# Softmax attention: the filler of the first head pair queued from step 0 over 22 steps, in place of from step 4 over 18

## The chip, the cores and the metric

The kernel runs on one core of one Trainium2 chip. The metric is the device time of one execution in microseconds (us). The engines are PE (TensorE, matrix products; PEld is its weight load), DVE (VectorE), ACT (ScalarE), POOL (GpSimd) and SP (SyncE, which here only issues DMAs).

## The reference

Two layers of a sequence model with 1024 channels and 16 + 1024 = 1040 positions, all in float32. A layer has a gated linear attention (GLA, 4 heads), a softmax attention with a forget gate (FoX, 8 heads of 64), one output projection, and a gated feed-forward part with a short convolution. The change touches only the order of work in the softmax attention, which computes for each head

```python
c = jnp.cumsum(log_f, axis=1)                      # forget bias per position and head
logits = q @ k.T / sqrt(64) + c[q_pos] - c[k_pos]  # causal: -inf where k_pos > q_pos
o_fox = softmax(logits) @ v                        # then a norm per head
```

Its q, k and v are columns of one input projection, x_normed @ w_in. The GLA output is multiplied by a gate, silu(x_normed @ w_gr), from four further column tiles of the same projection.

## The kernel before

Activations lie transposed: channels on partitions, positions along the free axis. Each float32 product is three matmuls on values split into a high and a low part (`mm3`, lines 222 to 224). Most large tiles live in 33 fixed slots of 128 x 1040 floats, handed out from a first-in first-out free list (`Slots`); a new user of a slot waits until the old one has been read for the last time. Two more slots exist during softmax attention, "lent", and only the low parts of k (`kL`) take them.

The instructions are written in program order; the layer that builds the program then orders each engine's queue by priority and readiness, so an instruction of a later place in the program can run earlier than one ahead of it. Each engine works its finished queue in order.

Within a layer's attention the order of the program is: the GLA stage for two pairs of heads (`gla_steps`; the products of the first softmax pair run between its steps, and the weights of the second pair's q tile are loaded there: `coming`), then `fox`. `fox` (line 769) walks 72 steps: four head pairs p, and for each five groups of query tiles (7,8), (5,6), (3,4), (1,2), (0), two heads e, and the tiles of the group. So a pair has 18 steps; steps 0 to 17 are pair 0, steps 18 to 35 pair 1. Tiles 8 and 7 have the longest rows of scores, so the first steps of a pair are the heaviest.

One step n issues the scores of its query tile (`fox_scores`: products S at L658 and L659, the running minimum over S plus bias on DVE at L661, the exponential P on ACT at L673), the transposes of P two steps later (`fox_transposes`, L694, split again into high and low parts at L336 and L337), the product with v three steps later (`fox_av`, L720), and the fold and store four and six steps later. `cb` (line 807) holds the forget bias of the two heads of a pair over all positions on all partitions; it is loaded by SP at the first step of a pair (L809) and masked by POOL (L838).

Between these, `work.run` issues pieces of other products, the filler. `plan(p)` puts it into a queue: for p from 0 to 2 the q, k and v projections of pair p + 1 (`fox_products`) and gate p (`gr_products`), each a weight tile of 128 columns with 3 chunks of positions (344, 348, 348) and 24 matmuls a chunk; the results of the matmuls are in tiles named mm. For p = 3 it is the last gate, and for p = 4 the first part of the output projection. `fox_products` takes eight slots when it is called (qA, kA, kL and V, two each). From pair 1 on, a plan begins four steps into its pair, because the slots of the pair before come free only there. The steps at which plans begin are in the list `starts`; the filler of a plan is cut evenly over the steps to the next start:

```python
            if p_next < 5 and n == starts[p_next]:
                work.drain()
...
                work = plan(p_next)
                p_next += 1
            fill_us = work.left / max(starts[p_next] - n, 1)
```

Weights of a tile arrive in two halves of 4 x 128 columns: SP loads them (L180, tile raw), ACT makes the high part (L189), POOL or DVE the low part (L191). The buffers for high and low parts are three each, so the second half of the next tile waits for the first half of the current one to be used for the last time. The accumulators mm are two; the score accumulators S are three.

Of the kernel before, what the change touches and what calls it, by code (L numbers as in the profile page):

```python
# [131 lines left out]
def mm_us(n):  # L132
    return max(n / 2400.0, 0.107) + 0.0025


class Kern:
# [632 lines left out]
    def fox(self, lyr, ap, pp, qs, plan, mix3):  # L769

        nc = self.nc
        groups = ((7, 8), (5, 6), (3, 4), (1, 2), (0,))
        steps = [(p, g, e, ti) for p in range(4) for g in range(5) for e in range(2)
                 for ti in reversed(range(len(groups[g])))]
        first = [steps.index((p, 0, 0, 1)) for p in range(4)]
        starts = [f + 4 for f in first] + [first[3] + 8, len(steps) + 8]
        cbs, state, due = {}, {}, {}
        work, p_next = plan(-1), 0  # L780

        def at(slot, kind, f):
            due.setdefault((slot, kind), []).append(f)

        def run(slot, kind):
            for f in due.pop((slot, kind), ()):
                f()

        for n in range(len(steps) + 8):
            if p_next < 5 and n == starts[p_next]:  # L790
                work.drain()
                if 0 < p_next < 4:
                    self.fox_free(qs[p_next - 1])
# [3 lines that stand above are left out]
            for kind in ('av0', 'T0'):  # L797
                run(n, kind)
            if n < len(steps):
                p, g, e, ti = steps[n]  # L800
                tiles = groups[g]
                i = tiles[ti]
                rows = self.rows_of(i)
                if g == 0 and e == 0 and ti == 1:
                    if p:
                        self.slots.put(*cbs[p - 1])
                    cbs[p] = [self.slots.get(F32, "cb") for _ in range(2)]
                    for x in range(2):
                        nc.sync.dma_start(cbs[p][x][:, :T],  # L809
                                          self.cd[2 * p + x:2 * p + x + 1, :].to_broadcast([128, T]))  # L810
                        self.fox_mask(cbs[p][x], NT - 1)
                if e == 0 and ti == len(tiles) - 1:
                    state[p, g] = {"den": ap.tile([128, 2, 2], F32, tag="den", name="den", bufs=3)}
                st = state[p, g]
                if ti == len(tiles) - 1:
                    st[e] = {}
                with self.tc.high_priority(8):
                    Ps = self.fox_scores(e, i, qs[p], cbs[p][e], st["den"][:rows, ti, e:e + 1], ap, pp)
                if i:
                    self.fox_mask(cbs[p][e], i - 1)  # L820
                self.fox_schedule(lyr, at, n, p, e, ti, i, tiles, Ps, st, qs[p], ap, pp, mix3)
            parts = [c for c in "12" if (n, "av" + c) in due or (n, "T" + c) in due]
            work.run(fill_us / (1 + len(parts)))
            run(n, "store")
            run(n, "fold")
            for c in parts:
                run(n, "av" + c)
                run(n, "T" + c)
                work.run(fill_us / (1 + len(parts)))
        work.drain()  # L830
        self.slots.put(*cbs[3])
        self.fox_free(qs[3])
# [52 lines left out]
    def attention(self, lyr, nm, hsrc, chunks, feed):  # L885
        tc, nc, s = self.tc, self.nc, self.slots
        with tc.tile_pool(name=f"aps{lyr}", bufs=2, space=PSUM, reuse_waits="tile") as pp2, \
# [7 lines left out]
            with tc.tile_pool(name=f"gla{lyr}", bufs=1, reuse_waits="tile") as gp:  # L895
# [33 lines left out]
                work = Work()  # L929
# [21 lines left out]
            with tc.tile_pool(name=f"att{lyr}", bufs=2, reuse_waits="tile") as ap, \  # L951
                    tc.tile_pool(name=f"lent{lyr}", bufs=1, reuse_waits="tile") as lp:
                s.lent = s.add(lp, 2, f"a{lyr}_")
                box = {}
                KORD = (4, 5, 0, 1, 2, 3, 6)

                def plan(p):
                    w = Work()
                    if p < 0:
                        return w  # L960
                    if p < 3:
                        self.fox_products(lyr, p + 1, w, ap, pp, nm, qs[p + 1], None if p else coming["w"])
                        self.gr_products(lyr, p, w, ap, pp, nm)
                    elif p == 3:
                        self.mixing = True
                        land = box["land"] = [s.get(F32, f"h{k}") for k in range(KD - 1)]
                        for k in (4, 5, 0, 1, 2):
                            nc.gpsimd.dma_start(land[k][:, :T], self.mixd[k][:])
                        self.gr_products(lyr, 3, w, ap, pp, nm, land[3])

                        box["wo"] = {"src": self.wm[lyr, M_WO], "slots": None}
                        w.boxes.append(box["wo"])
                    elif p == 4:
                        land = box["land"]
                        for c0, n in reversed(CH):
                            nc.gpsimd.dma_start(land[6][:, c0:c0 + n], self.mixd[6][:, c0:c0 + n])
                        for x in nm["x"]:
                            s.put(*x)
                        s.put(nm["r"])
                        mix = box["mix"] = [(s.get(F32R, f"mh{k}"), s.get(F32R, f"ml{k}")) for k in range(KD)]  # L980
                        hT = box["hT"] = land

                        own = box["own"] = [s.get(F32R, "wl", (128, KD, 128)) for _ in range(2)]
                        boxes = [{"src": self.wm[lyr, M_WO + m], "work": w, "slots": own if m % 2 else None}
                                 for m in range(NSPLIT)]
                        boxes[0]["w"] = box["wo"]["w"]
                        w.boxes += boxes

                        def split(j):
                            c0, n = CH[j]  # L990
                            for k in KORD:
                                self.split(mix[k][0][:, c0:c0 + n], mix[k][1][:, c0:c0 + n], land[k][:, c0:c0 + n])
                            for m in range(NSPLIT):
                                nc.gpsimd.dma_start(hT[m][:, c0:c0 + n], hsrc[m][:, c0:c0 + n])
                        split(2)
                        boxes[1]["w"] = self.weights(boxes[1]["src"], own)

                        def ev(m):
                            def f(ps, c0, n):
                                h = hT[m][:, c0:c0 + n]  # L1000
                                nc.vector.tensor_tensor(out=h, in0=ps, in1=h, op=ALU.add)
                            return f

                        before = {(1, 2): lambda: split(1), (1, 1): lambda: split(0)}
                        for m, j in [(m, j) for j in (2, 1, 0) for m in (0, 1)] + [(m, j) for m in (2, 3) for j in (2, 1, 0)]:
                            c0, n = chunks[j]
                            w.add(self.unit(pp, boxes[m], boxes[m]["src"], KORD, mix, c0, n, ev(m), before.get((m, j))),
                                  len(KORD) * 3 * mm_us(n))
                    return w
                self.fox(lyr, ap, pp, qs, plan, lambda: box["mix"][KD - 1])  # L1010
                s.put(*box["own"])
                box["hT"].append(s.get(F32, "h7"))
# [752 lines left out]
```

## Time and profile before

| what | us |
|---|---|
| median of 3 runs | 2517.86 (2516.19 to 2520.93) |
| the profiled execution's own time | 2518.04 |
| its span, first to last instruction | 2516.3 |
| PE busy in the span | 2477.9 |
| DVE busy | 1767.2 |
| ACT busy | 1272.9 |
| POOL busy | 385.3 |

The profile gives busy time for each engine; instructions that only wait, branch or issue DMAs do not count. The ends of matmuls are modelled, so rows of PE overlap and the start of the next row tells more than the end of the last. Softmax attention runs from about 175 to 496 us in layer 0 and from about 1419 to 1740 us in layer 1.

### The profile page before, as it was taken

Reading aid. Unit: us, or ns where it says so; the run is one execution under the profiler, and the core shown is the slowest. Engines: PE = TensorE matmul, PEld = TensorE weight load, DVE = VectorE, ACT = ScalarE, POOL = GpSimd, SP = SyncE. Lnnn points to the kernel's source line nnn. Section 1 sums busy time; section 2 is a strip of 40 time slices with the busy share of each in tenths; the row PEclk is TensorE's granted clock in tenths of the full one; section 3 lists DMA queues with packets and bytes.
Section 4 is the critical chain, followed back from the end, with each engine's and each line's share of the span. In section 5 each row is a group of like instructions: output and inputs, shape, how many; then the busy total and the mean of one; then the engine's idle time right before and its main releaser. Section 6 shows DMA issues by size and latency. Waiting matters only on the chain.

```text
span 2516.3 us, 47049 instructions
## 1 busy us (share of the span) xinstructions
PE 2477.9 (98%) x18442; PEld 2383.8 (95%) x18442; DVE 1767.2 (70%) x3523; ACT 1272.9 (51%) x2733; POOL 385.3 (15%) x567
## 2 busy tenths in 40 slices
PE   9999999999999999999999999999999999999998
PEld 8999999999999999999999899999999999997786
DVE  8656777769877777853666666777798777787535
ACT  7346666636544445631443566665464444455312
POOL 2023433210000000100211234331100000001002
PEclk9999999999999999999999999999999999999999
DMA  3232134343322224763312222143433222258722
GB/s 133 67 88 74 44 92 133 118 130 97 119 81 81 77 77 146 193 170 106 107 57 69 74 80 78 58 153 109 142 105 101 76 79 78 80 166 186 194 56 74
DMA packets 118542, 260.94 MB, mean 104 GB/s; under 512 B 14880, under 2 KB 32544, under 8 KB 118320
## 3 DMA queue, kind: packets, MB, share of 16 engines
q1 hardware_dynamic: 93984, 182.79, 23.5%
q0 software_dynamic: 22464, 72.84, 10.4%
q8 instruction: 144, 2.36, 0.4%
q10 hardware_dynamic: 1872, 2.31, 0.3%
q14 instruction: 78, 0.64, 0.1%
HBM read 177.29 MB, written 67.81 MB: 97 GB/s over the span
## 4 chain that ended last, share of the span: by engine, by line
PE 81%; DVE 10%; ACT 4%; DMA 2%; issue 2%; SPq 0%; POOL 0%; DVEq 0%; ACTq 0%; POOLq 0%
PE up L222 11%; PE up L224 11%; PE up L223 11%; PE mm L222 7%; PE mm L224 7%; PE mm L223 7%; PE down L222 5%; PE down L223 5%; PE down L224 5%; PE av L720 3%; PE tr L694 2%; DVE S L661 1%; PE S L658 1%; ACT P L673 1%; PE S L659 1%
## 5 line engine op out<-in xcount | busy, mean ns | idle before, releaser
L222 PE MATMUL up<-x,hi 128*128 128x260 f32 (+1 forms) x2464 | 696.6, 283 | 0.0
L224 PE MATMUL up<-x,hi 128*128 128x260 f32 (+1 forms) x2464 | 695.9, 282 | 0.7 <-DVE x L1097 0.7
L223 PE MATMUL up<-x,lo 128*128 128x260 f32 (+1 forms) x2464 | 696.3, 283 | 0.0
L224 PEld LDWEIGHTS up<-x,hi 128*128 128x128 f32 x2464 | 465.3, 189 | 1.1 <-DVE x L1097 1.1
L222 PEld LDWEIGHTS up<-x,hi 128*128 128x128 f32 x2464 | 464.5, 189 | 0.4 <-DVE hu L1263 0.2
L223 PEld LDWEIGHTS up<-x,lo 128*128 128x128 f32 x2464 | 464.5, 189 | 0.1
L1073 DVE TENSOR_TENSOR lo<-raw,hi 128x512 fp32r<-128x512 f32 x364 | 247.7, 685 | 173.0 <-ACT hi L1072 172.7
L222 PE MATMUL mm<-xh,hi 128*128 128x348 f32 (+4 forms) x1056 | 362.7, 343 | 0.0
L224 PE MATMUL mm<-xl,hi 128*128 128x348 f32 (+4 forms) x1056 | 339.8, 322 | 0.0
L223 PE MATMUL mm<-xh,lo 128*128 128x348 f32 (+4 forms) x1056 | 339.4, 321 | 0.0
L1072 ACT CAST hi<-raw 128x512 fp32r<-128x512 f32 x364 | 223.6, 620 | 128.1 <-PE up L224 84.5
L222 PEld LDWEIGHTS mm<-xh,hi 128*128 128x128 f32 x1056 | 199.5, 189 | 5.2 <-issue 4.6
L223 PEld LDWEIGHTS mm<-xh,lo 128*128 128x128 f32 x1056 | 199.5, 189 | 0.7 <-issue 0.7
L224 PEld LDWEIGHTS mm<-xl,hi 128*128 128x128 f32 x1056 | 198.3, 188 | 0.4 <-issue 0.3
L189 ACT CAST hi<-raw 128x512 fp32r<-128x512 f32 (+2 forms) x168 | 97.4, 581 | 176.0 <-PE down L224 97.0
L223 PE MATMUL down<-ah,lo 128*128 128x260 f32 (+1 forms) x528 | 168.6, 319 | 0.4 <-DVE lo L191 0.3
L224 PE MATMUL down<-al,hi 128*128 128x260 f32 (+1 forms) x528 | 168.5, 319 | 0.0
L222 PE MATMUL down<-ah,hi 128*128 128x260 f32 (+1 forms) x528 | 168.2, 319 | 0.0
L673 ACT ACTIVATE P<-S,m 116x460 f32<-116x460 f32 (+2 forms) x224 | 124.8, 561 | 71.2 <-DVE m L661 67.6
L337 DVE TENSOR_TENSOR PT<-tr,PT 116x464 fp32r<-116x464 f32 (+3 forms) x240 | 122.8, 514 | 46.9 <-ACT PT L336 45.3
L1055 DVE TENSOR_TENSOR raw<-raw,raw 128x512 f32<-128x512 f32 x198 | 129.4, 684 | 17.2 <-DMA raw<-in_wd_dram 16.5
L1288 POOL DMA_DIRECT2D actd<-cv x44 | 23.6, 535 | 756.9 <-DVE cv L1287 735.9
(289 smaller groups left out, 5623.8 us busy)
## 6 DMA issues: line engine op xcount, KB each, us to landing
raw<-in_wm_dram SPq DMA_DIRECT2D x330, 256.0 KB, 2.7
raw<-in_wd_dram SPq DMA_DIRECT2D x64, 256.0 KB, 3.6
actd<-cv POOLq DMA_DIRECT2D x22, 520.0 KB, 3.0
actd<-cv POOLq DMA_DIRECT2D x22, 512.0 KB, 2.9
cb<-cd SPq DMA_DIRECT2D x16, 520.0 KB, 4.1
st<-actd SPq DMA_DIRECT2D x14, 520.0 KB, 4.9
st<-actd SPq DMA_DIRECT2D x14, 512.0 KB, 4.6
kA<-kA SPq DMA_DIRECT2D x24, 260.0 KB, 3.9
```

What stands on the lines that cost most here:

```text
L189: nc.scalar.copy(hi[:, :n, :], raw[:, :n, :])
L222: nc.tensor.matmul(ps, wh, xh[:, c0:c0 + n], start=first, stop=False, skip_group_check=more)
L223: nc.tensor.matmul(ps, wl, xh[:, c0:c0 + n], start=False, stop=False, skip_group_check=more)
L224: nc.tensor.matmul(ps, wh, xl[:, c0:c0 + n], start=False, stop=last, skip_group_check=more)
L337: nc.vector.tensor_tensor(out=lo, in0=src, in1=hi.bitcast(F32), op=ALU.subtract)
L658: nc.tensor.matmul(S[:rows, :n], q["qA"][e][:, qs], q["kA"][e][:, c0:k1], start=True, stop=False)
L673: nc.scalar.activation(P[:rows, :n], S[:rows, :n], AF.Exp, scale=-1.0, bias=m[:rows, nch - 1:nch], accum_out=(den if nch == 1 else d3[:row ...
L694: nc.tensor.transpose(tr[:w, 3 - j, :rows], P[:rows, o:o + w], id_)
L720: nc.tensor.matmul(av[:, a:b], w.rearrange("p a b -> p (a b)"), x, start=(t == ts[0] and part == 0 and i == 0), stop=(t == last and i == 1))
L1055: nc.vector.tensor_tensor(out=q[out][:, :nk, :], in0=q[a][:, :nk, :], in1=q[b][:, :nk, :], op=op)
L1072: nc.scalar.copy(hi[:, :nk, :], src[:, :nk, :])
L1073: nc.vector.tensor_tensor(out=lo[:, :nk, :], in0=src[:, :nk, :], in1=hi[:, :nk, :].bitcast(F32), op=ALU.subtract)
```

## The change

The list of starts begins with step 0 in place of 4, and the empty plan that filled the first four steps is gone. So the q, k and v projections of pair 1 and the first gate are queued from step 0 on and spread over 22 steps in place of 18. As `plan(0)` is called at the top of step 0, it takes its slots before `cb` of pair 0 does. Every later plan begins where it did.

```diff
         first = [steps.index((p, 0, 0, 1)) for p in range(4)]
-        starts = [f + 4 for f in first] + [first[3] + 8, len(steps) + 8]
+        starts = [0] + [f + 4 for f in first[1:]] + [first[3] + 8, len(steps) + 8]
         cbs, state, due = {}, {}, {}
-        work, p_next = plan(-1), 0
+        work, p_next = Work(), 0
...
                 def plan(p):
                     w = Work()
-                    if p < 0:
-                        return w
                     if p < 3:
```

## The prediction

> **What bounds the kernel now.** I read the page's busy line and its chain, then the stages of the first head pair, then the waits of the stage that stands out.
>
> ```profile
> PE 2477.9 (98%) x18442; PEld 2383.8 (95%) x18442; DVE 1767.2 (70%) x3523; ACT 1272.9 (51%) x2733; POOL 385.3 (15%) x567
> PE 81%; DVE 10%; ACT 4%; DMA 2%; issue 2%; SPq 0%; POOL 0%; DVEq 0%; ACTq 0%; POOLq 0%
> ```
>
> TensorE is the bound: 98% busy, 81% of the chain. A change that moves matmuls and removes none can gain only where TensorE waits. So the question is how much it waits in the 22 steps over which the filler is now spread ("filler": what `plan(0)` queues, 4 tiles x 3 chunks x 24 = 288 matmuls). A step begins with the first score matmul (L658) of a query tile. Steps 0, 4, 8, 18, 22 and 26 of layer 0 begin here:
>
> ```profile
> 175.54 0.45 PE L658 MATMUL S<-kA,qA 128*116 128x460 f32 x1
> 192.14 0.37 PE L658 MATMUL S<-kA,qA 128*116 128x460 f32 x1
> 207.33 0.37 PE L658 MATMUL S<-kA,qA 128*116 128x460 f32 x1
> 249.01 0.42 PE L658 MATMUL S<-kA,qA 128*116 128x460 f32 x1
> 268.10 0.37 PE L658 MATMUL S<-kA,qA 128*116 128x460 f32 x1
> 289.15 0.37 PE L658 MATMUL S<-kA,qA 128*116 128x460 f32 x1
> ```
>
> The stretches between them by windows (length, then busy time and count of PE, PEld, DVE, ACT, POOL, then clock, DMA share, GB/s); the second fence holds the filler alone (the tile mm):
>
> ```profile
> 175.50:192.10 16.60, 16.25 (x103) 14.13 (x102) 10.94 (x37) 10.95 (x33) 5.50 (x8) 1.00 0.24 70
> 192.10:207.30 15.20, 13.75 (x104) 12.72 (x103) 10.76 (x35) 10.80 (x33) 4.02 (x7) 1.00 0.01 2
> 207.30:249.00 41.70, 41.41 (x300) 40.81 (x299) 23.91 (x81) 24.64 (x74) 17.30 (x22) 1.00 0.34 95
> 268.10:289.10 21.00, 21.00 (x155) 20.68 (x154) 16.26 (x51) 14.58 (x42) 9.15 (x14) 1.00 0.22 69
> ```
> ```profile
> 175.50:192.10 16.60, 9.07 (x50) 7.84 (x50) 1.53 (x3) 0.00 (x0) 1.00 0.24 70
> 192.10:207.30 15.20, 3.37 (x16) 2.59 (x16) 0.00 (x0) 0.00 (x0) 1.00 0.01 2
> 207.30:249.00 41.70, 30.12 (x159) 25.11 (x159) 3.58 (x7) 0.00 (x0) 1.00 0.34 95
> 249.00:268.10 19.10, 11.93 (x63) 9.93 (x63) 1.02 (x2) 0.00 (x0) 1.00 0.16 55
> 268.10:289.10 21.00, 13.22 (x66) 10.37 (x66) 1.52 (x3) 0.00 (x0) 1.00 0.22 69
> ```
>
> Two things stand out. 50 of the 288 filler matmuls already run in steps 0 to 3, though the program queues none before step 4: the instructions are reordered ahead of their place when TensorE is free. And the hole is in steps 4 to 7: only 16 filler matmuls, TensorE idle 15.20 - 13.75 = 1.45 us, while the same four query tiles of the second pair (steps 22 to 25) carry 66 and show no idle time. Layer 1 has the same stage again, to 0.01 us of PE:
>
> ```profile
> 175.50:216.70 41.20, 39.10 (x270) 35.62 (x269) 27.70 (x92) 28.97 (x85) 14.82 (x21) 1.00 0.14 42
> 1419.30:1460.50 41.20, 39.11 (x271) 35.60 (x269) 27.73 (x92) 28.94 (x85) 14.84 (x21) 1.00 0.13 42
> ```
>
> In the hole the scores wait for the exponentials that free their banks, with nothing else ready (waits of steps 4 to 7, then the timeline):
>
> ```profile
> PEld S L658 <- ACT P L673: 1.5, 2, 0.9
> PE S L658 <- ACT P L673: 1.1, 2, 0.7
> ```
> ```profile
> 194.81 0.42 PE L658 MATMUL S<-kA,qA 128*116 128x348 f32 x1 [0.75 <-ACT P L673]
> 196.99 0.47 PE L658 MATMUL S<-kA,qA 128*116 128x460 f32 x1 [0.37 <-ACT P L673]
> ```
>
> **The change part by part, per layer.** *(a) The fill rate.* No instruction is added or removed; 288 matmuls are spread over 22 steps (13.1 a step) in place of 18 (16). Two of them back to back:
>
> ```profile
> 149.79 0.32 PE L223 MATMUL mm<-xh,lo 128*128 128x348 f32 x1
> 149.95 0.32 PE L224 MATMUL mm<-xl,hi 128*128 128x348 f32 x1
> ```
>
> They start 0.16 us apart. Without filler, steps 4 to 7 take 15.20 - 16 x 0.16 = 12.64 us; steps 22 to 25 take 21.00 - 66 x 0.16 = 10.44. The hole costs 2.2 us. After the change these steps get about 52 filler matmuls. By a straight line between the two stages (2.2 us over 66 - 16 = 50 matmuls, 0.044 us each) 36 more recover 1.6; if 13 a step already hide all, 2.2. I take 2.0, nearer the upper end, because the idle rows above are single waits under 0.8 us, which five matmuls cover. Steps 0 to 3 get 52 in place of 50: nothing.
>
> *(b) The thinner end.* Steps 8 to 21 had 159 + 63 = 222 and keep 14 x 13.1 = 183, so 39 fewer. The nearest rows with thin filler are in the fourth pair (steps 12 to 15 of it, all engines, then filler), and the heaviest steps of these are 20 and 21 (third fence):
>
> ```profile
> 474.90:488.90 14.00, 14.00 (x96) 13.77 (x96) 9.92 (x32) 6.94 (x22) 2.78 (x6) 1.00 0.33 115
> ```
> ```profile
> 474.90:488.90 14.00, 10.45 (x48) 8.21 (x48) 1.19 (x3) 0.00 (x0) 1.00 0.33 115
> ```
>
> ```profile
> 257.10:268.10 11.00, 10.88 (x74) 9.62 (x72) 10.68 (x33) 9.50 (x31) 3.31 (x6) 1.00 0.10 34
> ```
>
> In the fourth pair 48 matmuls in four steps keep TensorE busy throughout, so 12 a step is enough on light steps. In steps 20 and 21 the vector engine is busy 10.68 of 11.00. Steps 18 to 21 lose 11 matmuls (63 to 52): nothing if covered, 11 x 0.044 = 0.5 us by the line, up to 1.7 (39 x 0.044) if the line held for all 14 steps. I take 0.3.
>
> *(c) What the moved steps carry along.* Three more weight tiles on SP's queue and their casts (ACT) and remainders (POOL), the splits of q, k and v, six copies of k on SP, the gate's loads (SP) and stores (POOL). Two neighbouring rows of SP's queue, and the cast of the second half of the k tile's weights:
>
> ```profile
> 177.94 1.78 SPq L615 DMA_DIRECT2D gog<-ogd  x2
> 209.13 4.93 SPq L180 DMA_DIRECT2D raw<-in_wm_dram  x2
> ```
> ```profile
> 207.12 0.62 ACT L189 CAST hi<-raw 128x512 fp32r<-128x512 f32 x1
> ```
>
> SP issues nothing from 179.72 to 209.13, POOL is busy 4.02 of 15.20 us in steps 4 to 7, ACT 10.80: room is there. That weight half is cast at 207.12, once the q tile, still running in the hole, frees its buffer; with the q tile earlier, this comes earlier too. Cost taken: 0; without that room, at most the hole of (a) again, 2.2 us; a gain beyond (a) is excluded, since no work goes away.
>
> *(d) The buffers change hands.* The loads of the forget-bias tiles `cb`, the last matmuls that read the second GLA pair's values (L505), SP's next row, the first reduction that reads `cb`, the time that its loads take to land, and its mask on POOL:
>
> ```profile
> 116.36 0.33 SPq L809 DMA_DIRECT2D cb<-cd  x1
> 123.12 0.33 SPq L809 DMA_DIRECT2D cb<-cd  x1
> ```
> ```profile
> 167.73 0.67 PE L505 MATMUL u<-gv,kd 64*64 64x128 f32 x16
> ```
> ```profile
> 169.96 0.46 SPq L584 DMA_DIRECT2D kL<-kL  x1
> ```
> ```profile
> 180.83 0.64 DVE L661 CUSTOM_DVE_ANT_0 S<-S,cb 116x460 f32<-116x460 f32 x1
> ```
> ```profile
> DMA to landing us min/median/max: 3.7/4.1/5.5
> ```
> ```profile
> 120.67 0.43 POOL L838 TENSOR_TENSOR cb<-cb,mask 116x116 f32<-116x116 f32 x1 [4.33 <-DMA cb<-cd]
> ```
>
> `plan(0)` now takes its six slots before `cb` takes its two. The free list holds, oldest first, four slots of the first GLA pair and four of the second. So far `cb` got the two oldest and was loaded at 116 and 123 us; now it gets the last two, the second pair's values, free at 168.4. Issued behind the copy of 169.96, the load lands at 170.4 + 4.1 and is masked by 175.0; the first reduction that reads it runs at 180.83, which is 5.8 us of cover. Cost 0, upper end in the rivals. Behind a waiting `cb` load on SP stand weight loads for the filler, which the buffers hold back anyway.
>
> **Sum.** 2.0 - 0.3 = 1.7 us a layer, 3.4 for two layers. The profiled execution took 2518.04 (span 2516.3), 0.2 above the median 2517.86; so 2514.6 against its own time and 2514.5 at the median, 0.14% faster. About 0.2% (5 us) is what a measurement can tell from no change.
>
> The Trainium skill (Perfetto Trace Analysis, Identifying the Most-Contended Engine) says that busy time of matmuls is a bad measure of headroom and that weight-load busy time should be used. By matmuls the hole is 1.45 us, by weight loads 15.20 - 12.72 = 2.48; the sum (a) would be 2.9 us for two layers by the one and 5.0 by the other, and the difference from the second pair's steps lies between, nearer the page's measure.
>
> **The rivals.** *All is recovered.* Steps 4 to 7 give 2.2, and the other idle time in reach too: 16.60 - 16.25 = 0.35 in steps 0 to 3, 41.70 - 41.41 = 0.29 in steps 8 to 17; nothing is given back. 2.8 a layer, 2512.2. For it: the second pair runs with almost no idle. Against: it has 16 matmuls a step, not 13.
>
> *The reordering has done it already.* If waits follow the straight line, 1.6 recovered is given back as 1.7 later: 2518. For it: 50 matmuls sit in steps 0 to 3 unasked. Against: the thin steps of the fourth pair.
>
> *The bias comes late (slower).* If its load is placed behind the weight and gate loads on SP, that is after 177.94 + 1.78 = 179.72, it is ready at 184.3, 3.4 us after 180.83; with a landing of 5.5, 4.8. It decides from an issue later than 176.3 on. Every softmax of the layer starts that much later with no filler left for the delay, minus the 1.7 gained: 1.7 to 3.1 a layer, 2521.3 to 2524.1, middle 2522.7. For it: SP does wait in order, as the loads of 116 and 123 us did for their slots. Against: SP's last copy leaves at 169.96, just after the slots come free.
>
> **How the numbers follow.** Chances: forecast 0.37, all recovered 0.28, done already 0.14, late bias 0.21. The forecast's own bounds are 2513 to 2517. Faster by over 0.2% (below 2512.8): the second case and a little of the first, 0.30. Slower by over 0.2% (above 2522.9): half of the late bias, and waits of the kind of (c) and (d) where I took zero, 0.22. Within: 0.48. The range reaches into both outer cases: 2511.5 to 2522.7.
>
> **What would show it.** In the changed profile the score matmul of step 8 should lie 3.8 us later after the first score (36 x 0.16 - 2.0) and that of step 22 1.7 us earlier; steps 4 to 7 should carry about 52 filler matmuls and idle under 0.4 us; steps 26 on should last as before; `cb` should be issued near 170 us, and L661 begin within 1 us of 180.8. Wrong is the prediction if `cb` is issued after 176, if steps 18 to 21 idle by more than 1 us, or if the reordering changes another stage.

## The result and the profile after

The changed kernel takes 2521.28 us (median of 13 runs, 2518.74 to 2526.64) against 2517.09 us (13 runs) before: a ratio of 1.0018, with a 95% interval of 1.0011 to 1.0026. By the medians it is 4.2 us slower. The forecast was 2514.5, so its sign was wrong, though 2521.28 lies inside the stated range. The profiled execution took 2522.45 us, with a span of 2520.4; of before, 2518.04 and 2516.3.

The page of the changed kernel, busy line and chain by engine:

```profile
PE 2476.4 (98%) x18442; PEld 2381.5 (94%) x18442; DVE 1773.2 (70%) x3523; ACT 1272.9 (51%) x2733; POOL 386.6 (15%) x567
PE 48%; issue 30%; DVE 13%; ACT 4%; DMA 3%; POOL 1%; SPq 0%; DVEq 0%; POOLq 0%; ACTq 0%
```

TensorE does the same work in the same time; what grew is the time around it. (30% of the chain now goes by "issue", time in which the engine waited for nothing that the profile shows. It says nothing of the loss: it is 30% in e15 too, the fastest of the kernels below.)

The stages of layer 0 in the changed kernel: steps 0 to 3, 4 to 7, 8 to 17, 18 to 21, and step 22 (length, then busy time and count of PE, PEld, DVE, ACT, POOL, then clock, DMA share, GB/s); the second fence holds the filler alone in the second to fourth of these stages.

```profile
174.24:192.95 18.71, 16.73 (x107) 14.78 (x105) 11.18 (x37) 11.25 (x34) 6.92 (x11) 1.00 0.30 92
192.95:212.39 19.44, 18.85 (x140) 18.32 (x138) 13.04 (x38) 13.91 (x39) 8.65 (x12) 1.00 0.10 30
212.39:250.34 37.95, 37.55 (x274) 36.48 (x272) 23.84 (x76) 21.23 (x67) 12.14 (x18) 1.00 0.36 91
250.34:267.56 17.22, 17.01 (x114) 15.39 (x113) 15.36 (x52) 13.44 (x46) 4.86 (x8) 1.00 0.19 59
267.56:274.48 6.92, 5.76 (x43) 5.42 (x42) 6.92 (x21) 4.35 (x14) 3.20 (x5) 1.00 0.45 147
```
```profile
192.95:212.39 19.44, 11.18 (x51) 8.11 (x51) 1.02 (x2) 0.00 (x0) 1.00 0.10 30
212.39:250.34 37.95, 25.70 (x132) 20.76 (x132) 2.56 (x5) 0.00 (x0) 1.00 0.36 91
250.34:267.56 17.22, 10.21 (x51) 8.11 (x51) 1.02 (x2) 0.00 (x0) 1.00 0.19 59
```

The change does what it says: steps 4 to 7 carry 51 filler matmuls in place of 16, and their idle time falls from 1.45 to 19.44 - 18.85 = 0.59 us. But two idle times are new: 18.71 - 16.73 = 1.98 us in steps 0 to 3, where it was 0.35, and 6.92 - 5.76 = 1.16 us in step 22, where it was none. The waits of PE in the two places (for whom; us, times, longest) name two different causes:

```profile
PE S L659 <- DMA kL<-kL: 1.8, 1, 1.8
PE S L658 <- ACT P L673: 1.2, 1, 1.2
```

**The first wait: the low part of k comes late.** The queue of SP and the first scores in the changed kernel:

```profile
165.29 0.46 SPq L584 DMA_DIRECT2D kA<-kA  x1
167.15 0.87 SPq L809 DMA_DIRECT2D cb<-cd  x1
168.26 0.78 SPq L584 DMA_DIRECT2D kL<-kL  x1
169.14 0.54 SPq L809 DMA_DIRECT2D cb<-cd  x1
```
```profile
174.24 0.45 PE L658 MATMUL S<-kA,qA 128*116 128x460 f32 x1
176.43 0.44 PE L659 MATMUL S<-kL,qA 128*116 128x460 f32 x1 [1.75 <-DMA kL<-kL]
```

The two `cb` loads now stand on either side of the last copy of kL. The copy is issued no later than before (6.0 us ahead of the first score; before, 175.54 - 169.96 = 5.6), but it lands much later. The transfers that the profile lists for the window of 168 to 178 us, with KB each and median us from issue to landing, in the changed kernel, and then the same copy in the kernel before:

```profile
cb<-cd SPq DMA_DIRECT2D x2, 520.0 KB, 8.2
raw<-in_wm_dram SPq DMA_DIRECT2D x3, 256.0 KB, 4.9
kL<-kL SPq DMA_DIRECT2D x1, 260.0 KB, 8.0
```
```profile
kL<-kL SPq DMA_DIRECT2D x1, 260.0 KB, 4.4
```

Before, the copy landed at 169.96 + 4.4 = 174.4 us, about 1.2 us ahead of the first score's start. That cover is what the change used up. In layer 1 the changed kernel shows the same wait with 0.3 us: there the copy landed after 6.4 us, and after 3.4 in the kernel before.

**The second wait: VectorE is behind at step 22.** The first reduction of step 22 (L661, 460 columns, on VectorE) frees the way for the exponential P that PE waits for. The first row is from the kernel before, the second from the changed one:

```profile
271.18 0.63 DVE L661 CUSTOM_DVE_ANT_0 S<-S,cb 116x460 f32<-116x460 f32 x1
```
```profile
271.73 0.63 DVE L661 CUSTOM_DVE_ANT_0 S<-S,cb 116x460 f32<-116x460 f32 x1
```

From the first score it starts 271.18 - 175.54 = 95.6 us later before, and 271.73 - 174.24 - 1.75 = 95.7 after, without the kL wait: VectorE arrives at the same moment, whatever PE had saved by then. It is busy all 6.92 us of that step.

Over steps 0 to 23 the changed kernel needs 105.31 us in layer 0 and 103.79 in layer 1, where the kernel before needs 103.06 and 102.98. Steps 24 to 35 are the same to 0.05 us. That is 3.1 us of the 4.1 by which the two spans differ. The rest has no one place: from step 36 of layer 0 to the first score of layer 1 (the rest of the attention, the feed-forward part and the next layer's start) it takes 3.6 us more, the time up to the first score is 1.3 us shorter and the time behind step 36 of layer 1 also 1.3. In the repeat below neither of the first two shows.

### The profile page after: what moved, and what is told of

It is laid out like the page before. It is cut to its first block, busy times and chain, and to the rows that moved or that the text cites. A ratio compares the mean times of both kernels' runs of the same rounds, so it can differ in the third digit from the quotient of the medians.

```text
span 2520.4 us, 47039 instructions
## 1 busy us (share of the span) xinstructions
PE 2476.4 (98%) x18442; PEld 2381.5 (94%) x18442; DVE 1773.2 (70%) x3523; ACT 1272.9 (51%) x2733; POOL 386.6 (15%) x567
## 4 chain that ended last, share of the span: by engine, by line
PE 48%; issue 30%; DVE 13%; ACT 4%; DMA 3%; POOL 1%; SPq 0%; DVEq 0%; POOLq 0%; ACTq 0%
PE mm L222 7%; PE mm L223 7%; PE mm L224 7%; PE down L223 5%; PE down L222 5%; PE down L224 5%; PE av L720 3%; PE tr L694 2%; DVE S L661 1%; PE S L658 1%; DVE x L1095 1%; PE S L659 1%; DVE cv L1254 1%; DMA kL<-kL 1%; DVE lo L1071 1%
```

## The experiments

All ratios are to the kernel before, measured beside the run on the same chip, with 95% intervals. "Steps 0 to 23" is the time from the first score of step 0 to that of step 24.

| run | median, us | ratio to before | steps 0 to 23, layer 0 / 1, us | steps 24 to 35, us |
|---|---|---|---|---|
| kernel before | | | 103.06 / 102.98 | 52.06 / 52.02 |
| changed, first profile | 2521.28 | 1.0018 [1.0011, 1.0026] | 105.31 / 103.79 | 52.11 / 51.99 |
| e0, changed again | 2521.88 | 1.0016 [1.0007, 1.0025] | 104.73 / 104.84 | 52.10 / 51.99 |
| e1, bias slots first | 2517.13 | 0.9999 [0.9990, 1.0008] | 103.52 / 103.54 | 52.04 / 51.97 |
| e2, before with late bias | 2521.12 | 1.0014 [1.0004, 1.0023] | 104.12 / 104.92 | 52.11 / 51.95 |
| e3, start at third step | 2516.74 | 0.9999 [0.9990, 1.0008] | 102.76 / 102.98 | 52.10 / 52.11 |
| e4, before, lean gate | 2515.78 | 0.9994 [0.9985, 1.0003] | 103.09 / 102.88 | 52.05 / 51.96 |
| e5, e1 with lean gate | 2515.52 | 0.9993 [0.9984, 1.0002] | 101.97 / 101.92 | 52.06 / 51.96 |
| e7, bias from POOL's queue | 2528.77 | 1.0042 [1.0028, 1.0055] | 109.78 / 109.90 | 52.13 / 51.97 |
| e8, gate second, 19 steps | 2523.73 | 1.0022 [1.0014, 1.0031] | 111.56 / 108.73 | 48.55 / 48.61 |
| e10, last gate chunk later | 2516.73 | 1.0000 [0.9991, 1.0009] | 102.77 / 102.80 | 52.40 / 52.35 |
| e11, splits of steps 0 to 21 on VectorE | 2516.98 | 0.9999 [0.9990, 1.0008] | 103.55 / 103.63 | 52.03 / 51.99 |
| e12, one bias late | 2520.17 | 1.0011 [1.0002, 1.0020] | 103.66 / 103.32 | 52.09 / 52.04 |
| e14, e1 with the turn's splits on VectorE | 2513.51 | 0.9989 [0.9980, 0.9998] | 101.95 / 101.88 | 52.22 / 52.18 |
| e15, e14 and e10 together | 2512.31 | 0.9985 [0.9976, 0.9993] | 102.18 / 102.18 | 51.89 / 51.85 |
| e16, before with the turn's splits on VectorE | 2517.54 | 1.0003 [0.9994, 1.0011] | 103.30 / 103.03 | 51.88 / 51.83 |
| e14 again | 2515.16 | 0.9991 [0.9982, 1.0000] | 102.03 / 101.92 | 52.27 / 52.21 |

### Once more (e0)

The changed kernel without an edit.

> The changed kernel once more, for a second profile. Theory (contention and VectorE): the time lies 3 to 5 us above the kernel before; steps 0 to 23 of layer 0 are 1.5 to 2.5 us longer than before, those of layer 1 0.3 to 1.0 us, and the wait of the first kL product (L659) of layer 0 is there again, 1 to 2 us. Rival (chance of one profile): the kL wait of layer 0 is below 0.5 us in this profile, and the longer stretches of the feed-forward part lie elsewhere than in the first profile.

The loss is there again, 1.0016. The kL wait is 1.2 us in layer 0 and 1.3 in layer 1, the stall of step 22 is 1.18 us in both. The longer stretch between the two softmax attentions is not there again: the window of 1000 to 1200 us, first in the first profile of the changed kernel, then in this one.

```profile
1000.00:1200.00 200.00, 195.06 (x1611) 194.44 (x1611) 115.37 (x146) 78.52 (x118) 14.77 (x18) 0.99 0.59 153
```
```profile
1000.00:1200.00 200.00, 197.27 (x1643) 196.65 (x1642) 117.76 (x149) 79.89 (x119) 14.74 (x18) 1.00 0.60 155
```

So what happens in this part differs from run to run, and the loss of steps 0 to 23 stays (3.5 us here, 3.1 in the first profile). How it falls on the two layers varies: 1.7 and 1.9 us here, 2.3 and 0.8 there; for layer 1 at most 1.0 us had been expected.

### The two parts of the change apart (e1, e2)

e1 keeps the new start and gives `cb` its old slots back:

```diff
         cbs, state, due = {}, {}, {}
+        cbs[0] = [self.slots.get(F32, "cb") for _ in range(2)]
...
                     if p:
                         self.slots.put(*cbs[p - 1])
-                    cbs[p] = [self.slots.get(F32, "cb") for _ in range(2)]
+                        cbs[p] = [self.slots.get(F32, "cb") for _ in range(2)]
```

e2 keeps the old start and gives `cb` the late slots:

```diff
-                    cbs[p] = [self.slots.get(F32, "cb") for _ in range(2)]
+                    late = [i for i in self.slots.free if i not in self.slots.lent][-2:] if p == 0 else [None] * 2
+                    cbs[p] = [self.slots.get(F32, "cb", first=[x]) for x in late]
```

> The changed kernel, but pair 0's two bias tiles take their slots ahead of the work's allocations, as in the kernel before, so that only the fill rate differs from the kernel before. Theory (the late bias loads delay the kL copies, and the slots' order spreads further): most of the loss is gone; the kL wait is below 0.3 us in both layers, the time lies between 1.0 us below and 1.5 us above the kernel before, and steps 0 to 23 are within 0.6 us of before in each layer. Rival A (the moved start itself costs: gate and products in the early steps): as slow as the changed kernel, 3 to 5 us above before. Rival B (the prediction as it was: the fill rate is worth 1.7 us per layer once the bias is early): 2.5 to 4 us below before.

> The kernel before, with its start at the fifth step, but pair 0's bias tiles take the last two free slots, those that the second gated-linear pair gives back; nothing else changes. Theory: 1.0 to 3.5 us above before, with a kL wait in step 0 of 0.3 to 2 us per layer. Rival A (the moved start itself costs): within 0.5 us of before. Rival C (the slots' order, through the feed-forward part's buffers too, is the whole of it): 3.5 to 5 us above before, with longer stretches in the feed-forward part as in the changed kernel.

e1 is as fast as the kernel before, e2 as slow as the changed kernel. Steps 0 to 23 of layer 0 and of layer 1, first in e1, then in e2:

```profile
176.12:279.64 103.52, 100.81 (x703) 95.21 (x701) 74.34 (x234) 67.95 (x208) 35.75 (x52) 1.00 0.26 72
1420.90:1524.44 103.54, 100.83 (x703) 95.14 (x701) 74.37 (x234) 67.93 (x208) 35.77 (x52) 1.00 0.26 73
```
```profile
175.96:280.08 104.12, 101.03 (x703) 95.34 (x702) 72.00 (x234) 68.00 (x207) 36.46 (x53) 1.00 0.26 77
1423.43:1528.35 104.92, 100.83 (x704) 95.30 (x703) 71.72 (x234) 67.97 (x207) 36.54 (x53) 1.00 0.25 76
```

In e2 the two layers lose 1.06 + 1.94 = 3.0 us, nearly all of it in step 0 (PE idles 1.0 and 2.1 us there, 0.23 before), and the time says 1.0014. In e1 step 0 idles 0.24 us as before, and the kL copy lands after 4.4 us again. (In layer 1 of e2 the profile puts PE's wait of 1.9 us down to a split on POOL. The product that waits reads nothing of that split; it reads kL, whose copy was issued at 1417.58 us and landed 8.0 us later, at 1425.6, and the product started at 1425.74.) So the late bias is the loss, and rival A of these two runs (the moved start) falls. Rival C (the slots' order acting through the feed-forward part) needs a second look, for in e2's profile the stretch from step 36 of layer 0 to layer 1's first score is 2.5 us longer than before. But it is 3.7 us longer in e10 below, where the bias is early, and no longer at all in e0, where it is late. It does not go with the slots, so this rival falls too. And the fill rate alone, which the prediction had priced at a gain of 1.7 us a layer, costs 0.5 us a layer in the trace: rival B falls too.

### How the loads delay the copy (e7, e12)

e7 is the changed kernel with pair 0's bias loads on another queue; e12 is the kernel before with one late bias tile.

```diff
-                        nc.sync.dma_start(cbs[p][x][:, :T],
-                                          self.cd[2 * p + x:2 * p + x + 1, :].to_broadcast([128, T]))
+                        (nc.sync if p else nc.gpsimd).dma_start(
+                            cbs[p][x][:, :T], self.cd[2 * p + x:2 * p + x + 1, :].to_broadcast([128, T]))
```
```diff
-                    cbs[p] = [self.slots.get(F32, "cb") for _ in range(2)]
+                    last = [i for i in self.slots.free if i not in self.slots.lent][-1] if p == 0 else None
+                    cbs[p] = [self.slots.get(F32, "cb", first=[i]) for i in (None, last)]
```

> The changed kernel with pair 0's two bias loads issued from POOL's queue in place of SP's; they still take the last two slots and still start late. Theory (the loads share the DMA engines' time with the kL copies, whoever issues them): the wait of the first kL product stays, 0.5 to 2 us per layer, and the time stays 2.5 to 5 us above before. Rival (the order of issues on SP makes the kL copies late): the wait is gone and the time is within 1.5 us of before.

> The kernel before, with only one of pair 0's two bias tiles on a late slot; it is issued ahead of the last kL copy, the other one stays early. Theory (the late loads and the kL copy share the DMA engines' time, in proportion to the bytes under way): the kL wait of step 0 is 0 to 1.0 us per layer, less than with both late (0.8 and 1.9 us), and the time 0 to 2 us above before. Rival (any load issued between the kL copies costs the whole wait): 0.8 to 2 us per layer, as with both.

On another queue it gets worse, not better: 1.0042. PE's wait in layer 0 of e7 and its transfers issued from 168 to 178 us:

```profile
PE S L659 <- DMA kL<-kL: 4.0, 1, 4.0
```
```profile
cb<-cd POOLq DMA_DIRECT2D x2, 520.0 KB, 10.1
raw<-in_wm_dram SPq DMA_DIRECT2D x2, 256.0 KB, 8.5
kL<-kL SPq DMA_DIRECT2D x1, 260.0 KB, 10.3
```

The copy is issued at the same place on SP with no bias load around it, and yet takes 10.3 us. So the order of issues on SP isn't the cause. What fits is that the transfers share what moves them. The Trainium skill says so (DMA: Bandwidth & Descriptors, Issuing engines are not separate DMA queues): whoever issues a transfer, all run on the same 16 engines and interleave. The trace agrees, and shows more than that: with the loads on the other queue the copy takes 2.3 to 3.3 us more than the 7.0 to 8.0 that it takes with them on SP.

The time rose by more than the 2.5 to 5 us that had been expected, and the copy alone doesn't make it. Steps 0 to 3 of layer 0 in e1, then in e7:

```profile
176.12:193.06 16.94, 16.67 (x108) 14.71 (x105) 11.18 (x37) 11.23 (x34) 6.08 (x9) 1.00 0.20 68
```
```profile
175.89:199.11 23.22, 19.19 (x108) 17.23 (x106) 11.34 (x37) 11.26 (x34) 6.94 (x11) 0.85 0.27 78
```

The same 108 matmuls keep PE busy 2.5 us longer, because the clock granted to TensorE is lower: 0.50 from 180 to 186 us, right behind the wait of 4.0 us, and 1.00 again from 188 us on. Layer 1 shows it again, with a wait of 4.8 us and 1.7 us more busy time. After the waits of at most 2 us in the changed kernel, e0 and e2 the granted clock stays at 1.00. So e7's loss is part wait and part clock, and only the wait bears on the queues.

With one late load (e12) the wait of layer 0 is 0.5 us and the copy lands after 6.6 us:

```profile
kL<-kL SPq DMA_DIRECT2D x1, 260.0 KB, 6.6
```

That is between 4.4 with none and 7.0 to 8.0 with two. In layer 1 it lands after 4.7 us, and the idle time of step 0 is 0.3 us, against 0.25 before. The rival of e12 (any load between the copies costs the whole wait) falls. Its time, 1.0011 or some 3 us, is more than the 2 us expected at most and than the 0.9 us that steps 0 to 23 show; its interval reaches down to 1.0002, and the rest isn't explained.

### A start at the third step (e3)

```diff
-        starts = [0] + [f + 4 for f in first[1:]] + [first[3] + 8, len(steps) + 8]
+        starts = [2] + [f + 4 for f in first[1:]] + [first[3] + 8, len(steps) + 8]
```

> The changed kernel with the start at the third step in place of the first (20 steps in place of 22), so that the bias tiles take their slots first by themselves. Theory: like the run with the bias slots first, between 1.0 us below and 1.5 us above before, with some 56 filler products in steps 4 to 7 and a stall of about 1 us on P in step 22. Rival A: 1.5 to 3.5 us above before, between the two kernels. Rival B: 2.5 to 4 us below before.

Here `cb` takes its slots first by itself, and the time is that of the kernel before. Steps 4 to 7 get only 37 filler matmuls and still idle 1.54 us, as the plan queued in step 2 runs from step 5 on; step 22 idles 0.0 and 0.16 us, not about 1. So the expectation of the time held and that of its make-up did not: little is won early, and little lost at step 22.

### What eats the gain at step 22 (e4, e5)

Both leave three VectorE instructions out of the first gate; e4 is the kernel before with that, e5 is e1 with that. (The last lines only give the result its right sign again.)

```diff
-            nc.vector.tensor_scalar(out=e, in0=x, scalar1=-87.0, scalar2=None, op0=ALU.max)
-            nc.scalar.activation(e, e, AF.Exp, scale=-1.0)
+            if h:
+                nc.vector.tensor_scalar(out=e, in0=x, scalar1=-87.0, scalar2=None, op0=ALU.max)
+            nc.scalar.activation(e, e if h else x, AF.Exp, scale=-1.0)
...
-            nc.vector.scalar_tensor_tensor(out=e, in0=e, scalar=1.0, in1=y, op0=ALU.add, op1=ALU.mult)
-            nc.vector.scalar_tensor_tensor(out=y, in0=e, scalar=-2.0, in1=y, op0=ALU.add, op1=ALU.mult)
+            if h:
+                nc.vector.scalar_tensor_tensor(out=e, in0=e, scalar=1.0, in1=y, op0=ALU.add, op1=ALU.mult)
+                nc.vector.scalar_tensor_tensor(out=y, in0=e, scalar=-2.0, in1=y, op0=ALU.add, op1=ALU.mult)
...
-            nc.vector.scalar_tensor_tensor(out=to, in0=y, scalar=-1.0, in1=og, op0=ALU.mult, op1=ALU.mult)
+            nc.vector.scalar_tensor_tensor(out=to, in0=y, scalar=-1.0 if h else 1.0, in1=og, op0=ALU.mult, op1=ALU.mult)
```

> The kernel before, with three VectorE instructions left out of the first gate of each layer (the clamp L621 and the two that refine the sigmoid, L626 and L627), nine per layer; the gate's last digits are thereby not the reference's. It is the base for the next run. Theory (PE sets the pace of steps 18 to 23 in the kernel before): steps 0 to 23 within 0.3 us of the kernel before in each layer, step 22 without PE idle, the time 0 to 1 us below before. Rival (VectorE already sets that pace in the kernel before): steps 18 to 23 are 1 to 3 us shorter per layer.

> The changed kernel with the bias slots first and the same three VectorE instructions left out of the first gate. Theory (in the kernel with the bias slots first, what steps 0 to 21 win is lost in step 22, where VectorE is behind with the gate's chain and PE waits for P): the PE idle of step 22 falls from 1.18 us to below 0.3 us, steps 0 to 23 take 102.0 to 102.7 us per layer, and the time is 1.0 to 2.5 us below the lean kernel before. Rival (the stall of step 22 is the thinner filling itself, a score product that waits for a bank whoever drains it): step 22 still idles 0.8 us or more and steps 0 to 23 still take 103.3 us or more.

Step 22 in e1, and then in e5:

```profile
267.70:274.60 6.90, 5.72 (x44) 5.39 (x42) 6.90 (x21) 4.36 (x14) 3.18 (x5) 1.00 0.47 147
```
```profile
267.30:272.86 5.56, 5.56 (x43) 5.51 (x42) 5.32 (x18) 5.18 (x17) 3.62 (x6) 1.00 0.38 109
```

In the kernel before, less VectorE work changes nothing (103.09 and 102.88 us): there PE sets the pace. In e5 the stall is gone and steps 0 to 23 take 101.97 and 101.92 us, 1.0 to 1.1 below e4. So what steps 0 to 21 win is real, and VectorE takes it back at step 22. The 1.0 to 2.5 us that e5 was expected to gain on e4 do not show in the medians (2515.78 and 2515.52); this reading rests on the trace.

### Remedies for step 22 (e8, e10, e11)

e8 puts the gate's tile second among the four tiles and the work on 19 steps, and issues what was put off to a next tile at the change of plans (`flush`); e10 puts the rest of the gate's third chunk off to the next tile; e11 moves the weight splits (L191) issued in steps 0 to 21 from POOL to VectorE. All three have the bias slots first.

```diff
-        starts = [0] + [f + 4 for f in first[1:]] + [first[3] + 8, len(steps) + 8]
+        starts = [0, first[1] + 1] + [f + 4 for f in first[2:]] + [first[3] + 8, len(steps) + 8]
...
+                self.flush()
...
+                        if p == 0:
+                            w.q[3:] = w.q[-3:] + w.q[3:-3]
+                            w.boxes.insert(1, w.boxes.pop())
```
```diff
+            def rest():
...
+            if h == 0 and c0 + n == T:
+                self.later.append(rest)
+            else:
+                rest()
```
```diff
-            eng = nc.gpsimd if self.att and not self.mixing else nc.vector
+            eng = nc.gpsimd if self.att and not self.mixing and not self.early else nc.vector
...
+            self.early = n < starts[1]
```

> A candidate: bias slots first, start at the first step, the gate's tile moved from fourth to second place in the work of pair 0, and this work spread over 19 steps, so that the products of pair 1 are still in time and the gate's VectorE chain lies in steps 4 to 9, where VectorE is some 70% busy. Theory (the gate's chain in steps 18 to 22 ate the gain): step 22's PE idle is below 0.3 us, steps 0 to 23 take 101.6 to 102.6 us per layer, the time is 1 to 3 us below before. Rival (any spread gives back at the thinner or later end what it wins): steps 0 to 23 at 102.9 us or more and a time within 1 us of before; the idle has moved to another step.

> The changed kernel with the bias slots first, and of the first gate's third chunk everything behind its evacuation (L621 to L631) is put off to the next tile's first chunk; nothing is left out. Theory (in step 22 the score's VectorE instruction L661 stands behind this chunk's chain): the PE idle of step 22 falls from 1.18 us to below 0.4 us, steps 0 to 23 take 102.0 to 102.9 us per layer, the time is 0 to 2.5 us below before. Rival (the idle only moves to step 23 or 24 with the chain): steps 0 to 27 together are no shorter than in the run with the bias slots first.

> The changed kernel with the bias slots first, and the weight splits L191 of steps 0 to 21 on VectorE in place of POOL. Theory (POOL's L191 lengthens the VectorE instruction that runs beside it: L627 took 1.45 us and L621 1.44 us there, 0.51 and 0.34 us elsewhere): both fall to 0.6 us or less; each split costs VectorE about 0.69 us, so that the step 22 stall shrinks by 0.3 to 1.0 us per layer, and steps 0 to 23 take 102.7 to 103.4 us. Rival (the lengthening has another cause, such as the state of PSUM or DMA traffic): L621 and L627 still show 1.4 us somewhere in steps 18 to 22, and step 22 idles more than 1.2 us, as VectorE has more to do.

e8 is slower, 1.0022: with the k tile third, pair 1's kL copies land too late for its first scores (PE waits 2.8 us for them in layer 0 and 1.4 in layer 1). The stall has left step 22 and changed its place. In steps 18 to 21 of layer 0, behind the longer wait, the granted clock is 0.93 and PE is busy 20.00 us, against 18.49 in layer 1 at 1.00, for 123 matmuls each. (Its steps 0 to 23 also hold more filler than the others', as pair 1's work begins in step 19; steps 0 to 35 take 160.1 and 157.3 us.)

e10 takes the stall out of step 22, but step 23 gets 0.5 us longer and steps 24 to 35 0.35 us a layer, and the time is that of the kernel before. Over steps 0 to 35 it is 0.4 us a layer shorter than e1 and no shorter than the kernel before.

e11 missed its aim. Steps 21 and 22 of it, first on VectorE, then on POOL:

```profile
266.57 1.45 DVE L627 SCALAR_TENSOR_TENSOR gy<-ge,gy 128x348 f32<-128x348 f32 x1
269.80 1.44 DVE L621 TENSOR_SCALAR ge<-gx 128x348 f32<-128x348 f32 x1
```
```profile
266.36 1.28 POOL L191 TENSOR_TENSOR lo<-raw,hi 128x512 fp32r<-128x512 f32 x1
269.74 1.30 POOL L191 TENSOR_TENSOR lo<-raw,hi 128x512 fp32r<-128x512 f32 x1
```

The two splits that run there belong to the next pair's first tile, are queued at step 22 and had not been moved. Both long VectorE instructions again stand beside one of them, so this run can't tell its theory from its rival.

### The splits of the turn (e14, e15, e16)

e14 moves exactly these splits, with the bias slots first; e15 adds the edit of e10; e16 is the kernel before with the moved splits alone.

```diff
-            eng = nc.gpsimd if self.att and not self.mixing else nc.vector
+            eng = nc.gpsimd if self.att and not self.mixing and not self.turn else nc.vector
...
+            self.turn = n == starts[1]
```

> The changed kernel with the bias slots first; of the weight splits L191 those that are issued with the next pair's first step (they ran at 266.6 and 269.9 on POOL in the run with the bias slots first) go to VectorE. Theory (POOL's split lengthens the VectorE instruction beside it): L627 and L621 of steps 21 and 22 fall from 1.45 and 1.44 us to 0.6 us or less, the first score instruction L661 of step 22 comes 1 to 2 us earlier after the first score, the PE idle of step 22 falls from 1.18 us to below 0.5 us and steps 0 to 23 take 102.2 to 103.0 us per layer. Rival (another cause for the long L621 and L627): both still take 1.4 us there, and the PE idle of step 22 stays above 1 us.

> A candidate: the run with the bias slots first, with both remedies of VectorE's queue at step 22: the splits of the next pair's first step on VectorE, and the rest of the first gate's third chunk put off to the next tile. Theory (without the delay at step 22 the filling of steps 4 to 7 is won): steps 0 to 35 take 154.0 to 155.1 us per layer, against 155.1 in the kernel before and 155.6 with the bias slots first, and the time is 0 to 2.5 us below before. Rival (what is put off is paid later): steps 0 to 35 at 155.1 us or more.

> The kernel before, start at the fifth step, with only the weight splits of the next pair's first step on VectorE. Theory (the early start is worth about 1.1 us per layer once VectorE is in time; the moved splits alone are worth nothing where PE already sets the pace): steps 0 to 23 take 102.7 to 103.1 us per layer, as in the kernel before, and the time is within 1.2 us of it. Rival (the gain of the last two runs is that of the splits, not of the early start): steps 0 to 23 take 101.7 to 102.5 us and the time is 1.5 us or more below before.

> The run with the bias slots first and the splits of the next pair's first step on VectorE, once more, on the same chip as the run above. Theory: steps 0 to 23 take 101.8 to 102.1 us per layer again, and the time is 1 to 3 us below before. Rival (its time was chance): within 0.8 us of before.

The same two instructions in e14, and the reduction of step 22 behind them; then steps 0 to 23 of both layers in e14, and of layer 1 in e16:

```profile
264.75 0.51 DVE L627 SCALAR_TENSOR_TENSOR gy<-ge,gy 128x348 f32<-128x348 f32 x1
267.29 0.33 DVE L621 TENSOR_SCALAR ge<-gx 128x348 f32<-128x348 f32 x1
268.04 0.64 DVE L661 CUSTOM_DVE_ANT_0 S<-S,cb 116x460 f32<-116x460 f32 x1
```
```profile
174.27:276.22 101.95, 100.45 (x703) 95.22 (x701) 73.04 (x236) 67.21 (x206) 32.02 (x48) 1.00 0.25 72
1418.77:1520.65 101.88, 100.38 (x703) 95.16 (x702) 72.58 (x237) 67.15 (x206) 31.57 (x48) 1.00 0.25 73
```
```profile
1420.65:1523.68 103.03, 100.77 (x704) 95.20 (x703) 72.04 (x237) 68.62 (x208) 32.31 (x49) 1.00 0.24 72
```

L627 falls from 1.45 to 0.51 us and L621 from 1.44 to 0.33, L661 of step 22 starts 268.04 - 174.27 = 93.8 us behind the first score in place of 95.7 in e1, and PE no longer waits in step 22. Steps 0 to 23 are 1.1 us a layer shorter than in the kernel before; the time is 0.9989 and, the second time, 0.9991, with an interval that reaches 1.0000. The moved splits alone (e16) make L627 and L621 just as short (0.51 and 0.34 us) and win nothing: 103.30 and 103.03 us, 1.0003. So both rivals fall: POOL's split does lengthen the VectorE instruction beside it, and the gain belongs to the early start, which needs VectorE to be in time.

e15 wins as much over steps 0 to 35 as e14 (154.1 and 154.0 us a layer, e14 154.2 and 154.1, kernel before 155.1 and 155.0). Its time, 2512.31 us and 0.9985, is the lowest of all runs, clear of the kernel before and of the changed one; from e14 it can't be told apart.

## Why the prediction was wrong

- *What bounds the kernel* was right: PE busy time is the same to 0.1% in the two kernels (2477.9 and 2476.4 us), and what changed is its idle time.
- *(a) The fill rate* was right in kind and over-sized. Steps 4 to 7 got 51 filler matmuls (52 forecast), and idle 0.59 us (under 0.4 forecast). Reckoned as the prediction reckons, at 0.16 us a matmul, they won 15.19 - (19.42 - 35 x 0.16) = 1.4 us in e1, where 2.0 was taken. (By idle time alone steps 0 to 7 won 0.9 us: 1.80 before, 0.27 + 0.60 = 0.87 in e1. The two differ because the modelled busy time shrinks too.) The comparison with steps 22 to 25 was not the fault: in e8 the same four steps carry 60 filler matmuls, don't idle, and win 15.19 - (20.01 - 44 x 0.16) = 2.2 us. The step that failed is to go above the straight line. The line gives 1.5 us for 35 matmuls more, and that is about what came; I took more because the waits seen were single ones under 0.8 us, and one of 0.6 us stayed. Of the two measures weighed there (the Trainium skill, Perfetto Trace Analysis, Identifying the Most-Contended Engine) the weight-load one, 2.48 us, is the nearer to the 2.2 of the fully filled hole in e8, as the prediction had it; with 51 matmuls that much doesn't come.
- *(b) The thinner end* was the second step that failed. The 39 matmuls fewer cost little where I looked for the cost: PE idles 0.1 us more in steps 8 to 17 and 0.1 us more in steps 18 to 21 (e1 against before); at 0.16 us a matmul these steps lost 0.7 us, where 0.3 was taken. The greater cost came one step further on, where nothing was thinned: step 22 has 16 filler matmuls in both kernels and became 1.35 us longer. I had the row that says why, VectorE busy 10.68 of 11.00 us in steps 20 and 21, and used it only to price missing filler. VectorE, 97% busy there, reached step 22 at the same time as before (95.6 and 95.7 us behind the first score), so that what PE had saved ahead of it was lost there. What holds VectorE up is a split on POOL beside L627 and beside L621: without the two, in e14, the loss is gone. In the kernel before, PE came late enough itself, and no wait was to be seen.
- *(c) What the moved steps carry along* holds: in steps 4 to 7 of the changed kernel PE waits once, 0.6 us, for P, as it did before (1.1 us there), and for none of the moved loads, casts or splits.
- *(d) The buffers change hands* is the step that turned the sign. Its readings were right: `cb` was issued at 167.15 and 169.14 us (near 170), and L661 of step 0 began at 181.28, within 1 us of 180.83. The error is in what the cover was measured for. I checked that the late load is in time for its own reader, 5.8 us, and took its landing time, 4.1 us, from the loads of the kernel before. I did not ask what else is in flight at 168 us: the last kL copy, whose cover was 1.2 us. That copy went from 4.4 to 8.0 us, the loads themselves from about 4 to 8.2. It cost 1.2 to 1.8 us a layer in three of four cases, and 0.3 in the fourth.
- *The rivals.* "The bias comes late" had the sign and nearly the time (2522.7), but not the mechanism: its load was issued at 169.14, not behind 179.72, and the first reader of `cb` did not wait for it. That the range took in the measured time is luck: it reached there for this rival. "The reordering has done it already" is near to what the fill rate did by itself in e1, though not by the straight line. "All is recovered" is refuted by the idle 0.59 us and by step 22.
- *What would show it.* Step 8 came 38.2 us after the first score, 6.4 later than before (3.8 forecast, and 1.75 of the kL wait on top); step 22 came 0.8 us later in place of 1.7 earlier, and in e1, without the wait, 1.0 earlier. Of the three signs of being wrong two stayed away (`cb` was issued before 176, and steps 18 to 21 idle 0.2 us); the third came, in step 22.

In sum, per layer: forecast + 2.0 - 0.3 = 1.7 us gain; found 0.9 of idle time won in steps 0 to 7, 0.2 lost in steps 8 to 21 and 1.2 in step 22, which makes the 0.5 us loss of e1, and 0.3 to 1.8 us more for the kL copies. With both losses removed, by the early bias and the moved splits of e14, steps 0 to 23 win 1.1 us a layer, and steps 24 to 35 give 0.2 back.

## What to carry to other kernels

When a change moves a transfer in time, look up what else is in flight there and how much cover each of those transfers has, not only whether the moved one reaches its own reader. Time saved on the bounding engine lasts only as far as the next place where a second engine, there nearly full, is in its way: look for the windows behind the saving in which another engine is over 95% busy. And where a hole is filled only in part, price it by the straight line between the measured stages, and above it only with a row that says so: here the line gave 1.5 us, 1.4 came, and 2.0 had been taken.

## What was not expected of the hardware

A POOL instruction on SBUF data can hold up a VectorE instruction for most of the POOL instruction's length: L621, 0.33 us by itself, took 1.44 us beside a split L191 of 1.30 us, and L627 1.45 in place of 0.51. Not every row suffers. In the changed kernel a reduction L661, with one of its inputs in PSUM, started inside a split and kept its 0.59 us, and so did a sum with a single SBUF input (L743, 0.42 us, begun at 289.74 inside the split of 289.46):

```profile
204.79 1.30 POOL L191 TENSOR_TENSOR lo<-raw,hi 128x512 fp32r<-128x512 f32 x1
```
```profile
204.91 0.59 DVE L661 CUSTOM_DVE_ANT_0 S<-S,cb,m 116x348 f32<-116x348 f32 x1
```

In the kernel before L627 took 1.45 us at the same place too; it cost nothing while PE was the later one. The Trainium skill states such a rule (SBUF — State Buffer, SBUF: two separate sides): VectorE and GpSimd share one pair of ports, which the first to start holds for its whole instruction while the other waits; on VectorE's side this holds for an instruction in a 2-port mode, or with two SBUF inputs beside a GpSimd instruction that reads SBUF. The runs e14 and e16 agree with it, in that the long rows go with the splits. L627 has two SBUF inputs; L621 has one, and no run here shows in which mode it runs.

The second is the size of the effect of one transfer on another: a copy of 260 KB landed after 4.4 us, after 6.6 with one load of 520 KB beside it, after 7.0 to 8.0 with two, and after 10.3 with the two on POOL's queue (all layer 0; in layer 1 3.4 to 3.8, 4.7, 6.4 to 8.0, and 9.4). Why the other queue is worse wasn't tried.

The third is the granted clock of e7 and e8: behind a wait of PE of 4.0 us it was 0.50 for some 6 us, behind one of 2.8 us it was 0.50 for some 2 us and 0.79 for the next 2, and behind waits of at most 2 us it stayed at 1.00. There a late copy costs more than the wait for it.
